# Four quarters of the array at once: a unit's second head pair beside its first

## The chip, the cores and the metric

The kernel runs on one core of a Trainium2 chip, as one program. Its time is the device time of that core in microseconds (us). TensorE has an array of 128 rows by 128 columns. A product whose operands lie on 64 partitions and whose result has 64 columns of weights uses one quarter of it: the rows are those of the operands' partitions, the columns decide on which partitions of PSUM the result lands. Which two quarters a pair of such products uses, and whether four products use all four, is what is changed here.

## The reference, cut to what matters

One layer of a decoder trunk for 256 prompt tokens and 32 sample tokens (8 sequences of 4). One input projection feeds 8 retention heads and 32 RWKV-7 heads of 64; one output projection follows. The change touches the RWKV-7 group only:

```python
def rwkv7_recurrence(r, w, k, v, kk, a, s0):
    def step(s, inp):
        r_t, w_t, k_t, v_t, kk_t, a_t = inp
        sa = jnp.einsum('bhvk,bhk->bhv', s, -kk_t)
        s = (s * w_t[:, :, None, :] + sa[..., None] * (kk_t * a_t)[:, :, None, :]
             + v_t[..., None] * k_t[:, :, None, :])
        return s, jnp.einsum('bhvk,bhk->bhv', s, r_t)
...
    o_rw, s_rwkv_new = rwkv7_recurrence(r_h, heads(decay), k_h, v_h, kk, heads(a), s_rwkv.astype(f32))
    o_rw = group_norm(o_rw, RWKV_GN_EPS) * ... + jnp.sum(r_h * k_h * r_k, axis=-1, keepdims=True) * v_h
```

Everything is float32.

## The kernel before

Three stretches follow one another: a front that computes the modulation (`ada`) and the normalised input, eight units that each hold the input projection of four RWKV heads and of one retention head, and the output projection. The projections are large products on the whole array (tile `acc`), with weights cut into a high and a low part (`whi` by ScalarE, `wlo` by VectorE or GpSimd) and three products a block.

A unit `q` of `rwkv_blocks` has two head pairs, `p` = 0 and 1. A pair's channels lie on the 128 partitions: head `h` = 0 on 0 to 63, `h` = 1 on 64 to 127 (`hs2`). The tokens are cut into nine chunks `c` of 32 (eight of the prompt, the ninth holds the sample tokens). The steps of a unit are generators that the planner interleaves with the projection's blocks:

- `main_gen`: builds `AR` and `BK` (channels on partitions), then the chunk products `scp` (line 838), whose masked result `SC` has tokens on partitions; turns `v` into token rows (`UV`, lines 849 to 854); the products `avp` (line 866) give `XR`.
- `inv_gen`: inverts the 32 by 32 triangles of the eight prompt chunks on VectorE, ended by the products `iva` and `ivb` (lines 961 to 974). `turn_gen` turns `BK` into token rows `BKt`.
- `chain_gen` (line 978): the recurrence over the eight prompt chunks, three groups of products a chunk in the tiles `ch` (`AR` by the state `S`, `WT` by `XR`, `BKt` by `UV`), for both pairs in each group.
- `sample_gen(p)` (line 1041), one for each pair: the ninth chunk with its eight states: `xps`, three times `ups`, `sps`.
- `out_gen` (line 1081): the products `ops` (line 1091), the norm of each head, and the turn back to channels, into `y`.

In all of these products head 0 reads partitions 0 to 63 (or a part of them) and writes PSUM partitions 0 to 63, and head 1 reads and writes 64 to 127, for both pairs: two quarters on a diagonal of the array. A float32 product on TensorE shows as two matmul records.

The order of the instructions is set when the program is built. `account` (line 196) keeps a simulated clock for each engine, and `c_pe` (line 212) gives each product's price; `tick` (line 287) lets a generator go on when its results are due by that clock, holds those that stopped at `PART` until two are held or one has waited 0.8 us, and lets `CHAIN` go at once. Each engine then runs its instructions strictly in that order. PSUM tiles come from three rings: `acc` (3 buffers), `tp` (3 buffers, `tps`), `ch` (2 buffers, used by the chain).

Of the kernel before, what the change touches and what calls it, by code (L numbers as in the profile page):

```python
# [10 lines left out]
F32 = mybir.dt.float32  # L11
# [6 lines left out]
P = 128  # L18
# [3 lines left out]
NB = 8  # L22
# [79 lines left out]
def tile_hybrid_step(  # L102
# [30 lines left out]

    def tt(eng, out, in0, in1, op):
        eng.tensor_tensor(out=out, in0=in0, in1=in1, op=op)
# [74 lines left out]
    small, weight = [False], [1.0]  # L210

    def c_pe(name, a, k):
        n, m, kk = free(a[0]), a[0].shape[0], a[1].shape[0]
        switch = 0.08 if small[0] and n >= 256 else 0.0
        small[0] = n < 128
        weight[0] = 0.3 if m <= 64 and kk <= 64 and n <= 64 else 1.0
        if m == 32 and n == 256 and kk == P:
            return 0.12 + switch
        passes, cyc = (1, 2) if name == "transpose" else (2, 2) if a[2].dtype == F32 else (1, 1)
        if m <= 64 and kk <= 64 and n == 512:  # L220
            return passes * 0.215
        if m <= 64 and kk <= 64 and n <= 64:
            return passes * (n * cyc / 2.4e3 + m / 2.4e3) / 2 + (0.02 if kk == 32 else 0.005 if passes == 2 else 0)
        return passes * (max(n * cyc / 2.4e3, m * 0.00084) + 0.0025) + switch
# [457 lines left out]
    def rwkv_blocks(q):  # L682
# [95 lines left out]
        def main_gen():  # L778
# [52 lines left out]
            flat = lambda t: t.rearrange("p a t -> p (a t)")  # L831
            for p in range(2):
                yield PART
                for c0, c1, m0 in ((0, 8, 0), (8, 9, 64)):
                    scp = tps("scp")
                    for c in range(c0, c1):
                        for h in hs2:
                            mm(scp[h, 64 * (c - c0):64 * (c - c0) + 64], flat(BK[h, p, c]), flat(AR[h, p, c]))
                    n = c1 - c0
                    tt(V, SC[:, p, c0:c1, :], scp[:, 0:64 * n].rearrange("p (c t) -> p c t", t=64),  # L840
                       mk[:, m0:m0 + 64].unsqueeze(1).to_broadcast([P, n, 64]), MUL)
                yield from pace(SPC)
# [6 lines left out]
            for p in range(2):  # L849
                V.transpose(UV[:, p, :, 32:64], c9(vw[:, p, :]))  # L850
                yield
                for h in range(2):
                    S.copy(UV[quad(h, 1), p, :, 0:32], UV[quad(h, 0), p, :, 32:64])
                yield
# [3 lines left out]
            B["XR"] = XR  # L858
            for p in range(2):
                yield PART  # L860
                for c0, c1 in ((0, 8), (8, 9)):
                    avp = tps("avp")
                    for c in range(c0, c1):
                        for h in hs2:
                            v = slice(h.start + 32, h.stop)
                            mm(avp[h, 64 * (c - c0):64 * (c - c0) + 64], SC[v, p, c, :], UV[v, p, c, :])
                    act(XR[:, p, c0:c1, :].rearrange("p c k -> p (c k)"), avp[:, 0:64 * (c1 - c0)], AF.Copy,
                        scale=K("amask"))
                yield from pace(SPC)
            yield from wait(("inv", q), ("bkt", q))  # L870
            B["s0"] = mx.tile([P, 2, NB, 64], F32, tag="b4", name="s0")
            B["xs"] = rwp.tile([P, 2, 64], F32, tag="MR", name="xs")
            for p in range(2):
                spawn(sample_gen(p), 2 + p)
            yield from chain_gen()
            yield from wait(("smp", q, 0), ("smp", q, 1), ("bps", q))
# [29 lines left out]
        def turn_gen(BK, BKt):  # L906
            for a in range(2):
                V.transpose(BKt[:, :, :, 32 * a:32 * a + 32], BK[:, :, :, a, :])
                yield
            for h in range(2):  # L910
                low, high = BKt[quad(h, 0), :, :, 32:64], BKt[quad(h, 1), :, :, 0:32]
                sw = B["zt"][96:128, 0:576].rearrange("t (p c k) -> t p c k", p=2, c=9)
                S.copy(sw, low)
                S.copy(low, high)
                S.copy(high, sw)
                yield
            flag(("bkt", q))
# [60 lines left out]
        def chain_gen():  # L978
# [5 lines left out]
            for c in range(NC):  # L984
                if c > 0:
                    for p in range(2):
                        for h in hs2:
                            mm(chs[p][h, 0:64], AR[h, p, c].rearrange("p a t -> p (a t)"), St[p][h, :])
                        tt(V, XR[:, p, c, :], chs[p][:, 0:64], XR[:, p, c, :], ADD)
                    yield CHAIN  # L990
                for p in range(2):
                    for a in ha2:
                        mm(chs[p][a, 64:128], WT[a, p, c, :], XR[a, p, c, :])
                    S.copy(UV[0:32, p, c, :], chs[p][0:32, 64:128])
                    V.tensor_copy(UV[64:96, p, c, :], chs[p][64:96, 64:128])
                yield CHAIN
                for p in range(2):
                    for h in hs2:
                        mm(chs[p][h, 128:192], BKt[h, p, c, :], UV[h, p, c, :])
                    sn = rwp.tile([P, 64], F32, tag=f"S{p}", name=f"S{p}", bufs=2)  # L1000
                    d = dec[p][:, c:c + 1]
                    if c == 0:
                        ts(V, sn, chs[p][:, 128:192], d, None, MUL)
                    else:
                        stt(sn, chs[p][:, 128:192], d, SP[p], MUL, ADD)
                    St[p] = sn
                    if c < NC - 1:
                        sp = rwp.tile([P, 64], F32, tag=f"SP{p}", name=f"SP{p}")
                        ts(V, sp, sn, dec[p][:, c + 1:c + 2], None, MUL)
                        SP[p] = sp  # L1010
                yield CHAIN
# [29 lines left out]
        def sample_gen(p):  # L1041
# [4 lines left out]
            s0r = B["s0r"][p]  # L1046
            s0, xs_, uvm = B["s0"][:, p], B["xs"][:, p], s0r.rearrange("p b v k -> p b (v k)")
            V.transpose(fl(s0), s0r.rearrange("p b v k -> p (b v k)"))
            yield PART
            xps = tps("xps")  # L1050
            for h in hs2:
                mm(xps[h], AR[h, p, 8].rearrange("p a t -> p (a t)"), fl(s0)[h])
            tt(V, uvm, xps.rearrange("p (b v) -> p b v", b=NB), bm, MUL)
            V.tensor_reduce(out=xs_, in_=uvm.rearrange("p b v -> p v b"), axis=AX.X, op=ADD)
            tt(V, XR[:, p, 8, :], XR[:, p, 8, :], xs_, ADD)
            tt(V, s0, s0, dec[p][:, 8:16].unsqueeze(2).to_broadcast([P, NB, 64]), MUL)
            yield PART
            for it in range(3):
                ups = tps("ups")
                src = XR if it == 0 else UV  # L1060
                for a in ha2:
                    mm(ups[a, 0:64], SC[a, p, 8, 0:CH], src[a, p, 8, :])
                for a in ha2:
                    tt(V, UV[a, p, 8, :], ups[a, 0:64], XR[a, p, 8, :], ADD)
                yield PART if it < 2 else None
            tt(G, uvm, UV[:, p, 8, :].unsqueeze(1).to_broadcast([P, NB, 64]), bm, MUL)
            yield PART
            sps = tps("sps")
            for h in hs2:
                mm(sps[h], BKt[h, p, 8, :], fl(uvm)[h])  # L1070
            tt(V, uvm, sps.rearrange("p (b v) -> p b v", b=NB),
               dec[p][:, 8:16].unsqueeze(2).to_broadcast([P, NB, 64]), MUL)
            yield
            tt(V, fl(s0), fl(s0), fl(uvm), ADD)
            yield
            V.transpose(s0r.rearrange("p b v k -> p (b v k)"), fl(s0))
            yield
            spawn(state_out(p, s0r))
            flag(("smp", q, p))

        def out_gen():
            SC, UV, XR = B["SC"], B["UV"], B["XR"]
            bst = rwp.tile([P, 18, 6], F32, tag="bst", name="bst")
            gst = rwp.tile([P, 3, 18], F32, tag="gst", name="gst")
            for p in range(2):
                yield PART
                for c0, c1 in ((0, 8), (8, 9)):
                    ops = tps("ops")
                    for c in range(c0, c1):
                        for h in hs2:  # L1090
                            mm(ops[h, 64 * (c - c0):64 * (c - c0) + 64], SC[h, p, c, :], UV[h, p, c, :])
                    xv = XR[:, p, c0:c1, :].rearrange("p c k -> p (c k)")
                    tt(V, xv, ops[:, 0:64 * (c1 - c0)], xv, ADD)
                yield from pace(SPC)
# [19 lines left out]
            for p in range(2):  # L1114
# [4 lines left out]
                for h in range(2):  # L1119
                    S.copy(o[quad(h, 0), :, 32:64], o[quad(h, 1), :, 0:32])  # L1120
                yield
                V.transpose(c9(on), o[:, :, 32:64])
# [434 lines left out]
```

## Time and profile before

| | |
|---|---|
| median of 3 runs | 1619.37 us (1618.7 to 1621.46) |
| the profiled execution's own time | 1622.13 us |
| its span, from the first to the last instruction | 1620.3 us |
| mean granted TensorE clock | 0.971 |
| TensorE, VectorE, ScalarE, GpSimd busy | 94%, 73%, 46%, 25% |

Busy time of an engine is the time in which at least one of its instructions was under way. Matmul records overlap, so the step from one start to the next says what a product costs, and its own duration does not. `x8` behind a row of the timeline is a count of records merged into it.

### The profile page before, as it was taken

The numbers are of one execution on the slowest core, as the hardware profiler recorded it, in microseconds if no ns is written. First come the engines' busy times: TensorE is split into PE (matmuls) and PEld (weight loads), VectorE is DVE, ScalarE is ACT, GpSimd is POOL, SyncE is SP. The second block draws the span as 40 slices with busy tenths as digits, with TensorE's granted clock in tenths as the row PEclk, the third lists the DMA queues.
The fourth block names the chain that finished last, engine by engine and source line by source line (L and its number), as shares of the span: only waits on it lengthen the run. The fifth ranks groups of instructions, "written<-read, shape, count | busy, mean of one in ns | idle before, by whom it ended". The sixth has DMA issues, their size and how long they took to land. (4 is left out here: it accounts for less than half of the span.)

```text
span 1620.3 us, 37403 instructions
## 1 busy us (share of the span) xinstructions
PE 1516.8 (94%) x14194; PEld 1341.9 (83%) x14194; DVE 1177.4 (73%) x2981; ACT 745.3 (46%) x1610; POOL 404.2 (25%) x425
## 2 busy tenths in 40 slices
PE   4889899999999999999999999999899999799996
PEld 2777897897889778878897898789878987699996
DVE  2434878998688869886888698878868986754544
ACT  2224453463446344534453455344543654454443
POOL 0001323422132214222412241324323422210100
PEclk8799999999999999999999999999999999999998
DMA  9995654664656456635674565365527543575553
GB/s 294 339 347 176 190 150 138 181 194 122 171 175 190 118 164 189 187 107 160 201 194 115 162 167 162 91 182 162 150 81 194 158 144 99 158 227 171 161 162 114
DMA packets 347761, 277.30 MB, mean 171 GB/s; under 512 B 90270, under 2 KB 346110, under 8 KB 346868
## 3 DMA queue, kind: packets, MB, share of 16 engines
q1 hardware_dynamic: 347580, 274.91, 58.4%
q8 instruction: 111, 1.82, 0.5%
q14 instruction: 70, 0.57, 0.1%
HBM read 248.80 MB, written 26.03 MB: 170 GB/s over the span
## 5 line engine op out<-in xcount | busy, mean ns | idle before, releaser
L249 PE MATMUL acc<-Hhi,whi 128*128 128x288 f32 (+2 forms) x2080 | 621.5, 313 | 17.2 <-DVE y L249 7.0
L249 PE MATMUL acc<-Hlo,whi 128*128 128x288 f32 (+2 forms) x2080 | 624.1, 311 | 0.0
L249 ACT CAST whi<-raw 128x512 fp32r<-128x512 f32 (+1 forms) x648 | 394.3, 617 | 404.9 <-PE acc L249 303.1
L249 PE MATMUL acc<-Hhi,wlo 128*128 128x288 f32 (+2 forms) x2080 | 458.6, 302 | 14.1 <-DVE wlo L249 13.4
L249 PEld LDWEIGHTS acc<-Hhi,whi 128*128 128x128 f32 (+1 forms) x2080 | 399.8, 192 | 52.5 <-issue 28.9
L249 POOL TENSOR_TENSOR wlo<-raw,whi 128x512 fp32r<-128x512 f32 x180 | 246.4, 1372 | 784.2 <-ACT whi L249 583.1
L249 DVE TENSOR_TENSOR wlo<-raw,whi 128x512 fp32r<-128x512 f32 (+1 forms) x468 | 337.2, 726 | 137.4 <-ACT whi L249 131.7
L249 PEld LDWEIGHTS acc<-Hlo,whi 128*128 128x128 f32 (+1 forms) x2080 | 399.5, 192 | 20.3 <-issue 8.1
L249 PEld LDWEIGHTS acc<-Hhi,wlo 128*128 128x128 f32 (+1 forms) x2080 | 341.9, 192 | 20.0 <-DVE wlo L249 18.3
L249 PE MATMUL acc<-yhi,whi 128*128 128x288 f32 x480 | 136.0, 299 | 7.4 <-ACT yhi L249 6.9
L249 PE MATMUL acc<-ylo,whi 128*128 128x288 f32 x480 | 136.0, 298 | 0.2 <-DVE ylo L249 0.2
L249 PE MATMUL acc<-yhi,wlo 128*128 128x288 f32 x480 | 101.4, 297 | 0.1
L249 PEld LDWEIGHTS acc<-yhi,whi 128*128 128x128 f32 x480 | 90.9, 189 | 8.1 <-ACT yhi L249 7.1
L249 PEld LDWEIGHTS acc<-ylo,whi 128*128 128x128 f32 x480 | 90.8, 189 | 0.7 <-DVE ylo L249 0.5
L249 PEld LDWEIGHTS acc<-yhi,wlo 128*128 128x128 f32 x480 | 76.8, 190 | 0.4 <-POOL wlo L249 0.3
L249 PE MATMUL adaps<-raw,cT 128*32 128x256 f32 x768 | 57.5, 419 | 7.2 <-DMA raw<-in_w_ada_dram 6.4
L249 DVE SCALAR_TENSOR_TENSOR s0b<-s0b,ups 128x512 f32<-128x512 f32 x64 | 40.9, 681 | 12.4 <-PE ups L249 12.4
L249 DVE SCALAR_TENSOR_TENSOR S<-ch,dec,SP 128x64 f32<-128x64 f32 x112 | 30.6, 279 | 24.7 <-PE ch L249 23.6
L249 PEld LDWEIGHTS adaps<-raw,cT 128*32 128x32 f32 x768 | 20.9, 116 | 30.4 <-DMA raw<-in_w_ada_dram 13.5
L249 ACT COPY UV<-ch 32x64 f32<-32x64 f32 x128 | 20.0, 198 | 53.6 <-PE ch L249 51.7
L249 DVE TENSOR_SCALAR SP<-S,dec 128x64 f32<-128x64 f32 x112 | 40.3, 360 | 4.0
L249 POOL TENSOR_TENSOR rot<-rot,rt 128x288 f32<-128x288 f32 x32 | 31.8, 1015 | 40.5 <-DVE rt L249 40.5
(250 smaller groups left out, 1989.4 us busy)
## 6 DMA issues: line engine op xcount, KB each, us to landing
raw<-in_w_in_dram SPq DMA_DIRECT2D x512, 256.0 KB, 2.9
raw<-in_w_ada_dram SPq DMA_DIRECT2D x64, 512.0 KB, 8.5
raw<-in_w_out_dram SPq DMA_DIRECT2D x128, 256.0 KB, 3.1
raw<-in_w_ada_dram SPq DMA_DIRECT2D x64, 256.0 KB, 3.1
s0b<-in_state_ret_dram SPq DMA_DIRECT2D x64, 256.0 KB, 4.3
out_dram<-s0b SPq DMA_DIRECT2D x64, 256.0 KB, 3.1
y<-in_x_prompt_dram SPq DMA_DIRECT2D x4, 1024.0 KB
s0r<-in_state_rwkv_dram SPq DMA_DIRECT2D x128, 32.0 KB, 2.8
```

What stands on the lines that cost most here:

```text
L249: return f(*a, **k)
```

## The change: the second pair takes the other diagonal

For `p` = 1 the token rows hold the heads in exchanged halves: head 0's tokens on partitions 64 to 127, head 1's on 0 to 63. A product from channels to tokens, or back, then has its operands on one half and its result on the other, so the second pair uses the other two quarters. `mm4` marks such products, and the planner's price of one is multiplied by 0.55. The two pairs' products of a step are issued together, in two banks. The other edits: `scp`, `avp` and `ops` take the two `ch` buffers and do both pairs in one step; the copies that put token rows in place are made anew (`turn_gen` builds the second pair's rows in `UV` as scratch, so `main_gen` waits for it before it fills `UV`); `sample_gen` does both pairs in one generator.

```diff
+    def mm4(out, lhsT, rhs):
+        four[0] = True
+        T.matmul(out, lhsT, rhs, start=True, stop=True)
+        four[0] = False
...
+        par = 0.55 if four[0] else 1.0
         if m <= 64 and kk <= 64 and n == 512:
-            return passes * 0.215
+            return par * passes * 0.215
...
-            for p in range(2):
-                yield PART
-                for c0, c1, m0 in ((0, 8, 0), (8, 9, 64)):
-                    scp = tps("scp")
-                    for c in range(c0, c1):
-                        for h in hs2:
-                            mm(scp[h, 64 * (c - c0):64 * (c - c0) + 64], flat(BK[h, p, c]), flat(AR[h, p, c]))
...
+            yield PART
+            scps, sc8 = [pch.tile([P, 512], F32, tag="ch", name="scp") for p in range(2)], [tps("scp") for p in range(2)]
+            for c in range(9):
+                for p in range(2):
+                    for h in range(2):
+                        o = hs2[h ^ p]
+                        t = scps[p][o, 64 * c:64 * c + 64] if c < 8 else sc8[p][o, 0:64]
+                        mm4(t, flat(BK[hs2[h], p, c]), flat(AR[hs2[h], p, c]))
...
-            for p in range(2):
-                V.transpose(UV[:, p, :, 32:64], c9(vw[:, p, :]))
-                yield
-                for h in range(2):
-                    S.copy(UV[quad(h, 1), p, :, 0:32], UV[quad(h, 0), p, :, 32:64])
+            yield from wait(("turn", q))
+            V.transpose(UV[:, 0, :, 32:64], c9(vw[:, 0, :]))
+            yield
+            for h in range(2):
+                S.copy(UV[quad(h, 1), 0, :, 0:32], UV[quad(h, 0), 0, :, 32:64])
+            yield
+            tq = rwp.tile([P, NR], F32, tag="tq", name="tq")
+            V.transpose(tq, vw[:, 1])
+            yield
+            for h in range(2):
+                for i in range(2):
+                    S.copy(UV[quad(1 - h, 1), 1, :, 32 * i:32 * i + 32], c9(tq)[quad(h, i)])
                 yield
...
+            avps, av8 = [pch.tile([P, 512], F32, tag="ch", name="avp") for p in range(2)], tps("avp")
...
         def turn_gen(BK, BKt):
+            T2 = B["UV"][:, 1]
             for a in range(2):
-                V.transpose(BKt[:, :, :, 32 * a:32 * a + 32], BK[:, :, :, a, :])
+                s = slice(32 * a, 32 * a + 32)
+                V.transpose(T2[:, :, s], BK[:, 1, :, a, :])
+                V.transpose(BKt[:, 0, :, s], BK[:, 0, :, a, :])
                 yield
             for h in range(2):
-                low, high = BKt[quad(h, 0), :, :, 32:64], BKt[quad(h, 1), :, :, 0:32]
-                sw = B["zt"][96:128, 0:576].rearrange("t (p c k) -> t p c k", p=2, c=9)
+                for i in range(2):
+                    for a in range(2):
+                        S.copy(BKt[quad(1 - h, a), 1, :, 32 * i:32 * i + 32], T2[quad(h, i), :, 32 * a:32 * a + 32])
+                    yield
+            flag(("turn", q))
+            for h in range(2):
+                low, high = BKt[quad(h, 0), 0, :, 32:64], BKt[quad(h, 1), 0, :, 0:32]
+                sw = c9(B["zt"][96:128, 0:288])
                 S.copy(sw, low)
                 S.copy(low, high)
                 S.copy(high, sw)
...
-                        for h in hs2:
-                            mm(chs[p][h, 0:64], AR[h, p, c].rearrange("p a t -> p (a t)"), St[p][h, :])
+                        for h in range(2):
+                            mm4(chs[p][hs2[h ^ p], 0:64], AR[hs2[h], p, c].rearrange("p a t -> p (a t)"), St[p][hs2[h], :])
+                    for p in range(2):
                         tt(V, XR[:, p, c, :], chs[p][:, 0:64], XR[:, p, c, :], ADD)
...
-                        mm(chs[p][a, 64:128], WT[a, p, c, :], XR[a, p, c, :])
+                        mm4(chs[p][a.start + 32 * p:a.stop + 32 * p, 64:128], WT[a, p, c, :], XR[a, p, c, :])
...
-                        mm(chs[p][h, 128:192], BKt[h, p, c, :], UV[h, p, c, :])
+                        mm4(chs[p][hs2[h ^ p], 128:192], BKt[hs2[h], p, c, :], UV[hs2[h], p, c, :])
...
-        def sample_gen(p):
+        def sample_gen():
...
+            xps = [tps("xps") for p in range(2)]
+            for p in range(2):
+                for h in range(2):
+                    mm4(xps[p][hs2[h ^ p]], AR[hs2[h], p, 8].rearrange("p a t -> p (a t)"), fl(s0s[:, p])[hs2[h]])
...
-                    mm(ups[a, 0:64], SC[a, p, 8, 0:CH], src[a, p, 8, :])
-                for a in ha2:
-                    tt(V, UV[a, p, 8, :], ups[a, 0:64], XR[a, p, 8, :], ADD)
+                    tt(V, UV[a, :, 8, :], ups[a, 0:128].rearrange("p (c v) -> p c v", c=2), XR[a, :, 8, :], ADD)
...
+            sps = [tps("sps") for p in range(2)]
...
+            ops, op8 = [pch.tile([P, 512], F32, tag="ch", name="ops") for p in range(2)], tps("ops")
...
                 for h in range(2):
-                    S.copy(o[quad(h, 0), :, 32:64], o[quad(h, 1), :, 0:32])
-                yield
-                V.transpose(c9(on), o[:, :, 32:64])
+                    S.copy(o[quad(h, 0), :, 32 - 32 * p:64 - 32 * p], o[quad(h ^ p, 1), :, 0:32])
+                yield
+                if p == 1:
+                    for h in range(2):
+                        S.copy(o[quad(h, 1), :, 0:32], o[quad(1 - h, 1), :, 32:64])
+                    yield
+                V.transpose(c9(on), o[:, :, 32 - 32 * p:64 - 32 * p])
```

The rows and counts of `avp`, `ups` and `ops` products stay as they were (`mm`, two quarters); only their grouping changes.

## Rows read from the trace of the kernel before

**Rows 1.** The page: busy us, share of the span and instructions of each engine.

```profile
PE 1516.8 (94%) x14194; PEld 1341.9 (83%) x14194; DVE 1177.4 (73%) x2981; ACT 745.3 (46%) x1610; POOL 404.2 (25%) x425
```

**Rows 2.** Busy time by stretch: the sixth unit, its chain, the stretch before a scp.

```profile
927.00:1082.00 155.00, 149.60 (x1469) 133.30 (x1464) 128.85 (x332) 76.87 (x163) 45.13 (x46) 1.00 0.55 153
...
1022.00:1074.00 52.00, 51.48 (x477) 40.09 (x474) 39.19 (x112) 20.98 (x58) 13.37 (x20) 1.00 0.45 119
...
1082.00:1124.00 42.00, 39.68 (x294) 38.46 (x291) 40.20 (x105) 18.74 (x34) 23.66 (x16) 0.96 0.60 165
```

**Rows 3.** Waits of TensorE, the longest kind: us in total, times, longest.

```profile
PE acc L249 <- DVE wlo L249: 13.4, 12, 3.0
```

**Rows 4.** Groups of TensorE's instructions by shape: count, busy, mean ns of one.

```profile
L249 PE MATMUL scp<-AR,BK 64*64 64x64 f32 x576 | 20.2, 221 | 0.0
...
L249 PE MATMUL xps<-s,AR 64*64 64x512 f32 x64 | 16.1, 592 | 0.0
```

**Rows 5.** Timeline of TensorE around one pair's scp: start, us.

```profile
1274.55 0.43 PE L249 MATMUL acc<-Hhi,wlo 128*128 128x288 f32 x2
1274.91 1.26 PE L249 MATMUL scp<-AR,BK 64*64 64x64 f32 x36
1276.10 0.40 PE L249 MATMUL acc<-Hhi,whi 128*128 128x288 f32 x1
1276.34 0.30 PE L249 MATMUL acc<-Hlo,whi 128*128 128x288 f32 x1
1276.47 0.30 PE L249 MATMUL acc<-Hhi,whi 128*128 128x288 f32 x1
```

**Rows 6.** Timeline of TensorE: a chain group, then an ups group.

```profile
1203.21 0.45 PE L249 MATMUL ch<-S,AR 64*64 64x64 f32 x8
1203.59 0.30 PE L249 MATMUL ups<-UV,SC 32*32 32x64 f32 x4
1203.82 0.40 PE L249 MATMUL acc<-Hlo,whi 128*128 128x296 f32 x1
```

**Rows 7.** Timeline of TensorE: both pairs' xps in one piece.

```profile
243.32 1.93 PE L249 MATMUL xps<-s,AR 64*64 64x512 f32 x8
245.19 0.40 PE L249 MATMUL acc<-Hlo,whi 128*128 128x288 f32 x1
```

**Rows 8.** Timeline of TensorE: retention products on column quarters, then row quarters.

```profile
272.31 1.07 PE L249 MATMUL rcr<-s0b,qp 128*32 128x256 f32 x16
273.19 0.61 PE L249 MATMUL rcr<-vf,scq 128*32 128x256 f32 x8
273.74 0.50 PE L249 MATMUL ups<-kv 32*128 32x256 f32 x4
274.17 0.40 PE L249 MATMUL acc<-Hhi,whi 128*128 128x296 f32 x1
```

**Rows 9.** The chain that ended last: start, us, what.

```profile
1151.61 1.19 PE avp L249 x36
...
1180.29 0.90 PE ivb L249 x64
...
1359.16 0.86 PE rop L249 x4
```

**Rows 10.** Groups of ScalarE and VectorE that the token rows take: busy us, mean ns.

```profile
L249 ACT COPY UV<-UV 32x288 f32<-32x288 f32 x32 | 13.8, 430 | 11.9 <-DVE UV L249 11.3
...
L249 ACT COPY BKt<-BKt 32x576 f32<-32x576 f32 x16 | 10.7, 671 | 0.5
...
L249 DVE TENSOR_TENSOR UV<-ups,XR 32x64 f32<-32x64 f32 x96 | 20.6, 215 | 1.7
...
L249 DVE STREAM_TRANSPOSE BKt<-BK 128x576 f32<-128x576 f32 x16 | 11.9, 746 | 0.0
...
L249 DVE STREAM_TRANSPOSE UV<-vw 128x288 f32<-128x288 f32 x16 | 7.5, 469 | 0.0
```

**Rows 11.** Timeline of VectorE behind the scp of rows 5.

```profile
1277.39 0.81 DVE L249 TENSOR_TENSOR SC<-scp,cst 128x512 f32<-128x512 f32 x2
```

More of the change, by code (lines that the diff above doesn't have):

```diff
@@ L208, in free @@
         return n
-    small, weight = [False], [1.0]
+    small, weight, four = [False], [1.0], [False]
     def c_pe(name, a, k):
@@ L219, in c_pe @@
         passes, cyc = (1, 2) if name == "transpose" else (2, 2) if a[2].dtype == F32 else (1, 1)
+        par = 0.55 if four[0] else 1.0
         if m <= 64 and kk <= 64 and n == 512:
-            return passes * 0.215
+            return par * passes * 0.215
         if m <= 64 and kk <= 64 and n <= 64:
-            return passes * (n * cyc / 2.4e3 + m / 2.4e3) / 2 + (0.02 if kk == 32 else 0.005 if passes == 2 else 0)
+            return par * passes * (n * cyc / 2.4e3 + m / 2.4e3) / 2 + (0.02 if kk == 32 else 0.005 if passes == 2 else 0)
         return passes * (max(n * cyc / 2.4e3, m * 0.00084) + 0.0025) + switch
@@ L831, in main_gen @@
             flat = lambda t: t.rearrange("p a t -> p (a t)")
-            for p in range(2):
-                yield PART
-                for c0, c1, m0 in ((0, 8, 0), (8, 9, 64)):
-                    scp = tps("scp")
-                    for c in range(c0, c1):
-                        for h in hs2:
-                            mm(scp[h, 64 * (c - c0):64 * (c - c0) + 64], flat(BK[h, p, c]), flat(AR[h, p, c]))
[L839 to L842, printed above, removed]
+            yield PART
[6 more added lines that the diff above has]
+                        mm4(t, flat(BK[hs2[h], p, c]), flat(AR[hs2[h], p, c]))
+            for p in range(2):
+                tt(V, SC[:, p, 0:8, :], scps[p].rearrange("p (c t) -> p c t", t=64),
+                   mk[:, 0:64].unsqueeze(1).to_broadcast([P, 8, 64]), MUL)
+                tt(V, SC[:, p, 8, :], sc8[p][:, 0:64], mk[:, 64:128], MUL)
+            yield from pace(SPC)
             B["zt"] = mx.tile([P, 1056], F32, tag="b4", name="zt")
@@ L858, in main_gen @@
             B["XR"] = XR
+            yield PART
+            avps, av8 = [pch.tile([P, 512], F32, tag="ch", name="avp") for p in range(2)], tps("avp")
             for p in range(2):
[L860 to L863, printed above, removed]
-                        for h in hs2:
[L865 to L869, printed above, removed]
+                for c in range(9):
+                    for h in hs2:
+                        v = slice(h.start + 32, h.stop)
+                        t = avps[p][h, 64 * c:64 * c + 64] if c < 8 else av8[h, 64 * p:64 * p + 64]
+                        mm(t, SC[v, p, c, :], UV[v, p, c, :])
+            for p in range(2):
+                act(XR[:, p, 0:8, :].rearrange("p c k -> p (c k)"), avps[p], AF.Copy, scale=K("amask"))
+            act(XR[:, :, 8, :], av8[:, 0:128].rearrange("p (a k) -> p a k", a=2), AF.Copy, scale=K("amask"))
+            yield from pace(SPC)
             yield from wait(("inv", q), ("bkt", q))
-            B["s0"] = mx.tile([P, 2, NB, 64], F32, tag="b4", name="s0")
-            B["xs"] = rwp.tile([P, 2, 64], F32, tag="MR", name="xs")
-            for p in range(2):
-                spawn(sample_gen(p), 2 + p)
+            spawn(sample_gen(), 2)
             yield from chain_gen()
-            yield from wait(("smp", q, 0), ("smp", q, 1), ("bps", q))
+            yield from wait(("smp", q), ("bps", q))
             yield from out_gen()
@@ L986, in chain_gen @@
                     for p in range(2):
-                        for h in hs2:
-                            mm(chs[p][h, 0:64], AR[h, p, c].rearrange("p a t -> p (a t)"), St[p][h, :])
+                        for h in range(2):
+                            mm4(chs[p][hs2[h ^ p], 0:64], AR[hs2[h], p, c].rearrange("p a t -> p (a t)"), St[p][hs2[h], :])
+                    for p in range(2):
                         tt(V, XR[:, p, c, :], chs[p][:, 0:64], XR[:, p, c, :], ADD)
@@ L992, in chain_gen @@
                     for a in ha2:
-                        mm(chs[p][a, 64:128], WT[a, p, c, :], XR[a, p, c, :])
-                    S.copy(UV[0:32, p, c, :], chs[p][0:32, 64:128])
-                    V.tensor_copy(UV[64:96, p, c, :], chs[p][64:96, 64:128])
+                        mm4(chs[p][a.start + 32 * p:a.stop + 32 * p, 64:128], WT[a, p, c, :], XR[a, p, c, :])
+                for p in range(2):
+                    S.copy(UV[0:32, p, c, :], chs[p][32 * p:32 * p + 32, 64:128])
+                    V.tensor_copy(UV[64:96, p, c, :], chs[p][64 + 32 * p:96 + 32 * p, 64:128])
                 yield CHAIN
                 for p in range(2):
-                    for h in hs2:
-                        mm(chs[p][h, 128:192], BKt[h, p, c, :], UV[h, p, c, :])
+                    for h in range(2):
+                        mm4(chs[p][hs2[h ^ p], 128:192], BKt[hs2[h], p, c, :], UV[hs2[h], p, c, :])
+                for p in range(2):
                     sn = rwp.tile([P, 64], F32, tag=f"S{p}", name=f"S{p}", bufs=2)
@@ L1045, in sample_gen @@
             fl = lambda t: t.rearrange("p b v -> p (b v)")
-            s0r = B["s0r"][p]
-            s0, xs_, uvm = B["s0"][:, p], B["xs"][:, p], s0r.rearrange("p b v k -> p b (v k)")
-            V.transpose(fl(s0), s0r.rearrange("p b v k -> p (b v k)"))
-            yield PART
[L1050 to L1056, printed above, removed]
+            ob = lambda t: t.rearrange("p (b v) -> p b v", b=NB)
+            s0s = mx.tile([P, 2, NB, 64], F32, tag="b4", name="s0")
+            xs_ = rwp.tile([P, 2, 64], F32, tag="MR", name="xs")
+            uvm = [t.rearrange("p b v k -> p b (v k)") for t in B["s0r"]]
+            dcs = [dec[p][:, 8:16].unsqueeze(2).to_broadcast([P, NB, 64]) for p in range(2)]
+            for p in range(2):
+                V.transpose(fl(s0s[:, p]), fl(uvm[p]))
+                yield
+            yield PART
+            xps = [tps("xps") for p in range(2)]
+            for p in range(2):
+                for h in range(2):
+                    mm4(xps[p][hs2[h ^ p]], AR[hs2[h], p, 8].rearrange("p a t -> p (a t)"), fl(s0s[:, p])[hs2[h]])
+            for p in range(2):
+                tt(V, uvm[p], ob(xps[p]), bm, MUL)
+            yield
+            for p in range(2):
+                V.tensor_reduce(out=xs_[:, p], in_=uvm[p].rearrange("p b v -> p v b"), axis=AX.X, op=ADD)
+                yield
+            tt(V, XR[:, :, 8, :], XR[:, :, 8, :], xs_, ADD)
             yield PART
@@ L1060, in sample_gen @@
                 src = XR if it == 0 else UV
+                for p in range(2):
+                    for a in ha2:
+                        mm(ups[a, 64 * p:64 * p + 64], SC[a, p, 8, 0:CH], src[a, p, 8, :])
                 for a in ha2:
-                    mm(ups[a, 0:64], SC[a, p, 8, 0:CH], src[a, p, 8, :])
-                for a in ha2:
-                    tt(V, UV[a, p, 8, :], ups[a, 0:64], XR[a, p, 8, :], ADD)
+                    tt(V, UV[a, :, 8, :], ups[a, 0:128].rearrange("p (c v) -> p c v", c=2), XR[a, :, 8, :], ADD)
                 yield PART if it < 2 else None
-            tt(G, uvm, UV[:, p, 8, :].unsqueeze(1).to_broadcast([P, NB, 64]), bm, MUL)
+            for p in range(2):
+                tt(G, uvm[p], UV[:, p, 8, :].unsqueeze(1).to_broadcast([P, NB, 64]), bm, MUL)
+                tt(V, s0s[:, p], s0s[:, p], dcs[p], MUL)
+                yield
             yield PART
[L1068 to L1072, printed above, removed]
-            yield
-            tt(V, fl(s0), fl(s0), fl(uvm), ADD)
-            yield
[L1076 to L1079, printed above, removed]
+            sps = [tps("sps") for p in range(2)]
+            for p in range(2):
+                for h in range(2):
+                    mm4(sps[p][hs2[h ^ p]], BKt[hs2[h], p, 8, :], fl(uvm[p])[hs2[h]])
+            for p in range(2):
+                tt(V, uvm[p], ob(sps[p]), dcs[p], MUL)
+            yield
+            for p in range(2):
+                tt(V, s0s[:, p], s0s[:, p], uvm[p], ADD)
+                yield
+                V.transpose(fl(uvm[p]), fl(s0s[:, p]))
+                yield
+                spawn(state_out(p, B["s0r"][p]))
+            flag(("smp", q))
         def out_gen():
@@ L1084, in out_gen @@
             gst = rwp.tile([P, 3, 18], F32, tag="gst", name="gst")
+            yield PART
+            ops, op8 = [pch.tile([P, 512], F32, tag="ch", name="ops") for p in range(2)], tps("ops")
             for p in range(2):
[L1086 to L1094, printed above, removed]
+                for c in range(9):
+                    for h in hs2:
+                        t = ops[p][h, 64 * c:64 * c + 64] if c < 8 else op8[h, 64 * p:64 * p + 64]
+                        mm(t, SC[h, p, c, :], UV[h, p, c, :])
+            for p in range(2):
+                xv = XR[:, p, 0:8, :].rearrange("p c k -> p (c k)")
+                tt(V, xv, ops[p], xv, ADD)
+            tt(V, XR[:, :, 8, :], op8[:, 0:128].rearrange("p (a k) -> p a k", a=2), XR[:, :, 8, :], ADD)
+            yield from pace(SPC)
             flag(("ops", q))
@@ L1119, in out_gen @@
                 for h in range(2):
-                    S.copy(o[quad(h, 0), :, 32:64], o[quad(h, 1), :, 0:32])
+                    S.copy(o[quad(h, 0), :, 32 - 32 * p:64 - 32 * p], o[quad(h ^ p, 1), :, 0:32])
                 yield
-                V.transpose(c9(on), o[:, :, 32:64])
+                if p == 1:
+                    for h in range(2):
+                        S.copy(o[quad(h, 1), :, 0:32], o[quad(1 - h, 1), :, 32:64])
+                    yield
+                V.transpose(c9(on), o[:, :, 32 - 32 * p:64 - 32 * p])
                 yield
```

## Prediction

> **What bounds the kernel now.** I read the page first: TensorE is busy 94% of the span, VectorE 73%, ScalarE 46% [rows 1]. Then the busy time by stretch: in a unit of 155 us TensorE has work under way for 149.6 us and VectorE for 128.9; in that unit's chain, where the touched products are, it is 51.5 and 39.2 of 52 us [rows 2]. The waits of TensorE agree: the longest kind, for the low part of the weights, is 13.4 us in all [rows 3]. So TensorE, which runs its queue in order, sets the time, and a step that it no longer spends is gained as long as VectorE keeps up. It nearly doesn't ahead of a `scp` (40.2 of 42 us, [rows 2]), but no product of the change lies there.
>
> **What a round costs.** The shapes show that the touched products use a quarter each and come as records of 64 columns (`scp`, 576 of them) or of 512 (`xps`, 64 of them) [rows 4]. From one group's start to the next group's: 36 records of `scp` take 1.19 us (1274.91 to 1276.10) [rows 5], 8 records of a chain group 0.38 (1203.21 to 1203.59) [rows 6]. Both have the same entry and exit, so the 14 rounds of two records between them cost 0.81 us: a round of two is 0.058 us, and 0.148 us a group is fixed. For `xps`, 8 records take 1.87 us [rows 7]; less 0.148, a round of two is 0.43 us. Do two records really share a round? A float32 record of 256 columns on the whole array takes 0.86 / 4 = 0.215 us (`rop`, [rows 9]), so 512 columns take 0.43: yes, the round of two costs what one record does.
>
> **Would four share it?** No row has four quarters of 64 by 64. The two things that are new have a row each. Two products on the same rows: `rcr` has four records at a time on all 128 rows in four column strips, 16 of them in 0.88 us, 0.22 for four of 256 columns [rows 8], the price of one. Two products that write the same PSUM partitions, in two banks: the retention's `ups`, 32 rows by all 128 columns, take 0.43 us for four records up to the next start [rows 8]. An `acc` record takes 0.13 for 288 columns (1276.34 to 1276.47, [rows 5]), so four of 256 columns in turn would need 0.46 without entry and exit; two at a time need 0.23, and leave 0.20 for these. So both kinds overlap, and I take full overlap: a round of four costs 0.058, or 0.43 for the long ones. The other end is no overlap, nothing gained a round.
>
> Nor does issue forbid it: `ivb` has 64 records, each with a weight load, in 0.90 us, 14 ns a record [rows 9], so four need 56 ns, just under the round of 58. The Trainium skill speaks against this point: in "TensorE: Matmul & The Clock Gate", Back-to-back issue gap, a matmul of up to 64 columns has a floor of about 25 ns, by which a round of four would take 0.100 us and save 0.016 of the two rounds' 0.116, not 0.058; the short rounds below would then save 8 us in all in place of 30, and the sum would end at 1598 us. The 14 ns of the row contradict that floor.
>
> **The sum, a unit.** Rounds saved: `scp` has 9 chunks for two pairs, 36 rounds of two, then 18 of four: 18. The chain groups go from 4 rounds to 2: 7 chunks with `AR`, 8 with `WT`, 8 with `BKt`: 14 + 16 + 16. That is 64 rounds by 0.058 = 3.71 us. `xps` and `sps` go from 4 long rounds to 2 each: 4 by 0.43 = 1.72. `scp`, `avp` and `ops` each go into the projection's stream once in place of twice. Such an insertion costs, beside its rounds, 0.10 on the way in (two `acc` records from 1274.55 would end their steps at 1274.81; `scp` starts at 1274.91), the fixed 0.148 and 0.11 on the way out (the first `acc` step is 0.24, later ones 0.13) [rows 5]: 0.36, three times 1.08. The sample's `ups` go from six groups to three; a group of 4 records takes 0.23, of which two rounds are 0.116 [rows 6], so 0.114 falls away three times: 0.34. Together 6.85 us a unit, 54.8 us for eight.
>
> **What it adds.** ScalarE, a unit: before, 8 copies of 288 columns at 0.43 and 6 of 576 at 0.67, 7.5 us; after, 6 for `UV`, 14 in `turn_gen`, 6 in the output at 0.43, 11.2 us [rows 10]; 3.7 more, 30 us in all, on an engine with 875 us free [rows 1]. What is late is `avp`: it now stands behind 8 of the copies, four turns of 0.47 and two more copies in `UV`, 6.2 us. It is covered by the inversion, which the chain needs too: an `avp` that starts at 1151.6 has 27.5 us from its end to the `ivb` at 1180.3 [rows 9]. I take 0; uncovered it would be 6.2 by 8 = 50 us. VectorE, a unit: four turns at 0.47 for two at 0.75 add 0.39; six fewer `ups` sums at 0.215, with the rest twice as wide, give back between 0 and 1.29 [rows 10]. Nothing either way.
>
> Two costs are waits of which the trace before has no row. First, the same work of VectorE falls into less time: 128.9 of 155 us become 128.9 of 148, 83% to 87% [rows 2]. Below, this costs nothing, since the chain's stretch has 13 us of VectorE free and loses 5 or less; above, I allow 2 us a unit; I take 1, 8 us in all. Second, the last chunk of `scp`, the `xps` and the `sps` now hold two of the three `tp` buffers at once. The products behind them in TensorE's queue, the retention's and the projection's alike, wait if they need a third. A buffer is held from the end of `scp` (1276.10, [rows 5]) to the end of its masking (1277.39 + 0.81, [rows 11]), 2.1 us; three such places in eight units are 50 us if each wait is whole, 0 if the third buffer does. Because other steps take one buffer at a time, I take 0.5 us a unit, 4 us.
>
> 54.8 - 8 - 4 = 42.8. The profiled execution took 1622.1 us (1620.3 of span and 1.8 around it), so 1579.3; it stands 2.8 above the median of the runs shown, so **1577 us** at their level. Its own range is 1562 (no added wait, and a few us for an order that the planner, with other prices, makes anew) to 1594 (30 us of added waits).
>
> **The rivals.**
>
> *The quarters take turns.* If two products on one half of the rows or of the PSUM partitions can't run together once all four quarters are in use, the 64 short and 4 long rounds save nothing. There remain 1.08 + 0.34 a unit, 11 us, less some 6 of added waits: 1614. Against it are rows 8, each for one half of the condition; no row has both. The Trainium skill would have it so: "TensorEngine Tiling (Array Packing)", Restrictions and Gotchas, says that different row tiles can't access the same PSUM bank simultaneously, and here both row halves write each bank. The trace disagrees already before the change: the two heads of a `scp` are two row halves that write one bank, and share a round of 0.058.
>
> *Issue binds.* If a record needs not 14 but 28 ns, four take what two rounds took, and only the long rounds and the insertions are left: 1.72 + 1.42 a unit, 25 us, less 12: 1606. Rows 9 speak against it, though 56 against 58 ns leaves little.
>
> *The waits eat half.* Full overlap, but `tp` buffers and VectorE cost 35 us in place of 12: 1600. For it: VectorE's 87%, and a planner that knows of no buffers. Against it: 13.4 us for the largest wait now [rows 3].
>
> *Slower: a change of diagonal drains the array.* A change of shape costs some 0.10 us [rows 5]. If going from one diagonal to the other counts as one, then each of a unit's 34 groups of eight records (9 + 7 + 8 + 8 + 1 + 1) pays at least twice: 68 by 0.10 is 6.8 us, less 1.42, plus 1.5 of waits, 55 us in eight units: 1674. The 1.42 and the waits cancel, so it decides from 0.006 us a change on (3 us in eight units). Against it: in rows 8 neither four column strips nor two row strips pay anything between them.
>
> **How the numbers follow.** Forecast 0.68 (1577), waits eat half 0.14 (1600), turns 0.09 (1614), issue 0.05 (1606), slower 0.04 (1674). The range 1560 to 1606 leaves out the turns, the slower case and the tails, under 0.2. A measurement of this kernel tells 0.2%, some 3 us, from no change. Faster: the first, second and fourth whole, and half of the third, 0.92; same 0.04, the rest of the third; slower 0.04.
>
> **What would show it.** One `scp` group of 72 records a unit from start to next start in about 1.2 us (2.2 if they take turns), with four records starting within some 25 ns and the next four 58 ns later; chain groups of 8 records at 0.26 us in place of 0.38; `xps` of 8 records at 1.0 in place of 1.87; `acc` records as many and as long as before. Wrong would be: TensorE waiting at `adat`, `rtp` or `rop` for a `tp` buffer behind `xps`; `avp` ending later than `ivb`; a granted clock under 1.0 in more stretches than before [rows 2], since the pauses between shorter groups stay.

## The result and the profile after

The changed kernel took 1579.2 us in the median (1576.7 to 1585.1) against 1620.4 before, a ratio of 0.975 with a 95% interval of 0.972 to 0.978: faster by 2.5%. The forecast was 1577.

The new rounds first. TensorE's timeline around the `scp` of the sixth unit, around a chain group and around `xps`, to be read beside [rows 5 to 7]:

```profile
952.00 0.29 PE L255 MATMUL acc<-Hhi,whi 128*128 128x288 f32 x1
952.23 1.28 PE L255 MATMUL scp<-AR,BK 64*64 64x64 f32 x72
953.43 0.40 PE L255 MATMUL acc<-Hlo,whi 128*128 128x288 f32 x1
...
241.98 0.34 PE L255 MATMUL ch<-S,AR 64*64 64x64 f32 x8
242.25 0.40 PE L255 MATMUL acc<-Hhi,whi 128*128 128x288 f32 x1
...
391.18 0.34 PE L255 MATMUL ch<-S,AR 64*64 64x64 f32 x8
391.34 1.04 PE L255 MATMUL xps<-s,AR 64*64 64x512 f32 x8
392.31 0.40 PE L255 MATMUL acc<-Hhi,whi 128*128 128x288 f32 x1
```

72 records of `scp` take 1.20 us from start to next start (36 took 1.19), 8 chain records 0.27 (0.38), 8 `xps` records 0.97 (1.87). Inside the first group four records start within 20 ns; the second four start 106 ns after the first, and from there on a round follows every 58 ns. So a round of four costs what a round of two did.

Now the balance. The page's first row and the cores' row of the kernel after:

```profile
PE 1473.6 (93%) x14194; PEld 1311.4 (83%) x14194; DVE 1170.0 (74%) x2899; ACT 777.7 (49%) x1698; POOL 442.8 (28%) x459
```
```profile
core 0: 1583.3 us, clock 0.967
```

Idle time of TensorE is span less busy time. What the granted clock withheld is the span by 1 less the mean clock. Busy time less that is called step time here: what the products would keep TensorE busy at full clock (pauses shorter than a record, some 0.2 us, hide in it).

| profiled execution | span | idle | withheld | step time |
|---|---|---|---|---|
| before | 1620.3 | 103.5 | 47.0 | 1469.8 |
| after | 1583.3 | 109.7 | 52.2 | 1421.4 |

So in this pair 48.4 us of step time went, and 11.4 came back: 6.2 as waits, 5.2 as clock. Two things limit this reading.

- It charges the clock also with time at 1.2 GHz in which TensorE had nothing to do (9 to 10 us of it behind the last product). TensorE was busy in 76.3 us of the time at 1.2 GHz before and in 79.9 after; its products lost half of that, 38.1 and 40.0. By this strict count 44.9 us of step time went, 6.2 came back as waits and 1.8 as clock. Kernels with the same products on the same quarters lie up to 8 us apart in step time by the first count and up to 3 by the strict one, so the strict figure is added below where it matters.
- The profiled execution after was the slowest of its four. The withheld time by the first count is 50.1 us in the mean of these four, and 50.4 in the mean of 33 executions of the kernel before that were timed beside the experiments. So over all executions the clock took nothing back that can be told.

TensorE's longest waits, where [rows 3] had 13.4 us for the low parts of the weights, and one that became shorter (here us in total, times, longest):

```profile
PE acc L255 <- DVE wlo L255: 22.5, 24, 2.6
PE acc L255 <- ACT yhi L255: 10.4, 1, 10.4
PE ch L255 <- DVE XR L255: 1.3, 3, 0.7
```

The same two waits in the kernel before:

```profile
PE ch L249 <- DVE XR L249: 8.9, 12, 1.8
PE acc L249 <- ACT yhi L249: 6.9, 1, 6.9
```

The wait for `yhi` stands where the output projection needs the result `y` of the last unit.

How the clock stood behind a wait is seen in the busy time by stretch of the kernel after. The last columns are the granted clock, the share of the DMA engines and GB/s:

```profile
660.00:670.00 10.00, 6.78 (x46) 4.99 (x44) 8.63 (x19) 5.88 (x13) 3.27 (x3) 0.99 0.62 190
670.00:682.00 12.00, 12.00 (x112) 11.86 (x113) 7.16 (x17) 3.55 (x7) 0.00 (x0) 0.58 0.32 89
```

TensorE had work for 6.8 of 10 us (one wait of 2.4 us, at an `adat`), and then ran most of the next 12 us at 1.2 GHz of 2.4.

### The profile page after: what moved, and what is told of

Read it like the earlier page. It is cut to its first block, busy times and chain, and to the rows that moved or that the text cites. A ratio compares the mean times of both kernels' runs of the same rounds, so it can differ in the third digit from the quotient of the medians.

```text
span 1583.3 us, 37468 instructions
## 1 busy us (share of the span) xinstructions
PE 1473.6 (93%) x14194; PEld 1311.4 (83%) x14194; DVE 1170.0 (74%) x2899; ACT 777.7 (49%) x1698; POOL 442.8 (28%) x459
## 5 line engine op out<-in xcount | busy, mean ns | idle before, releaser
L255 PE MATMUL acc<-Hlo,whi 128*128 128x288 f32 (+2 forms) x2080 | 617.7, 309 | 0.0
L255 POOL TENSOR_TENSOR wlo<-raw,whi 128x512 fp32r<-128x512 f32 x214 | 290.6, 1361 | 753.2 <-ACT whi L255 524.7
L255 PEld LDWEIGHTS acc<-Hlo,whi 128*128 128x128 f32 (+1 forms) x2080 | 399.4, 192 | 14.6 <-issue 5.7
L255 DVE TENSOR_TENSOR wlo<-raw,whi 128x512 fp32r<-128x512 f32 (+1 forms) x434 | 315.1, 731 | 126.9 <-ACT whi L255 122.3
L255 DVE COPY UV<-ch 32x64 f32<-32x64 f32 x128 | 28.9, 226 | 31.9 <-ACT UV L255 28.7
L255 ACT COPY UV<-ch 32x64 f32<-32x64 f32 x128 | 25.5, 199 | 41.4 <-PE ch L255 39.7
L255 DVE TENSOR_SCALAR SP<-S,dec 128x64 f32<-128x64 f32 x112 | 38.1, 340 | 4.0
```

What stands on the lines that cost most here:

```text
L255: return f(*a, **k)
```

## The experiments

Each was timed several times over, in turn with the kernel before (medians 1622.6 to 1623.0 there). Ratios are to it, with their 95% intervals. "Strictly" marks step time by the strict count.

**one_diagonal: the same order, without the quarters.**

```diff
-                        o = hs2[h ^ p]
+                        o = hs2[h]
...
-                            mm4(chs[p][hs2[h ^ p], 0:64], AR[hs2[h], p, c]...
+                            mm4(chs[p][hs2[h], 0:64], AR[hs2[h], p, c]...
```
and alike for `WT`, `BKt`, `xps` and `sps`.

> The changed kernel with its grouping, copies and order of instructions kept to the letter, but every mm4 product of the second pair put in the first pair's quarters (the planner's prices kept too). The second pair's results are then not those of the reference. Overlap theory (four quarters at once make the gain): 64 short rounds by 0.058 us and 4 long ones by 0.43 come back in each of eight units, 43 us; 1579 + 43 = 1622 us, with chain groups of 8 records at 0.38 us again and xps of 8 records at 1.85. Rival (the grouping, fewer insertions and fewer changes of shape, makes the gain and the quarters take turns): within 5 us of the changed kernel, 1574 to 1584.

1605.4 us, 0.989 (0.987 to 0.991). Neither number: 26 us above the changed kernel, where the theory had 43 and the rival under 5. The order is the same: in the two traces the same instructions follow one another on every engine (all but 4 of TensorE's 14194 records). The rounds themselves did come back, as its timeline shows (72 records of `scp` in 2.24 us):

```profile
965.33 2.31 PE L255 MATMUL scp<-AR,BK 64*64 64x64 f32 x72
967.57 0.40 PE L255 MATMUL acc<-Hlo,whi 128*128 128x288 f32 x1
```

Its page and cores' row, and its first wait:

```profile
PE 1501.8 (94%) x14194; PEld 1337.0 (83%) x14194; DVE 1167.1 (73%) x2899; ACT 771.8 (48%) x1698; POOL 444.0 (28%) x459
```
```profile
core 0: 1602.6 us, clock 0.969
```
```profile
PE acc L255 <- DVE wlo L255: 17.7, 21, 2.6
```

Step time 1452.1, so the quarters take away 30.7 us (strictly 32.1); idle 100.8 against 109.7, so 8.9 of that came back as waits.

**grouping_alone: the other half of the change, as a kernel.** `o = hs2[h]` and alike, the copies and turns of the kernel before, price 1.0; the grouping kept.

> The grouping without the quarters, as a kernel of its own that computes the reference: both pairs in one step of scp, avp, ops and of the sample, but the second pair's token rows, copies and quarters as before, and the planner's prices as before. Overlap theory: 1.42 us a unit for insertions and ups groups, 11 us, less some waits for tp buffers; 1609 to 1617 us. Rival (grouping makes the gain): 1575 to 1590.

1608.7 us, 0.991 (0.989 to 0.993): at the lower end of the theory's range, 14.0 us below the kernel before. Its page and cores' row:

```profile
PE 1506.8 (94%) x14194; PEld 1340.9 (84%) x14194; DVE 1176.7 (73%) x2901; ACT 744.9 (46%) x1602; POOL 432.7 (27%) x441
```
```profile
core 0: 1605.4 us, clock 0.966
```

Step time 1506.8 busy less 54.6 withheld = 1452.2, the same as one_diagonal's; the grouping takes away 17.6 us (strictly 15.1), more than the 11.4 of the sum.

**long_rounds_back: only xps and sps return.**

```diff
-                    mm4(xps[p][hs2[h ^ p]], ...
+                    mm4(xps[p][hs2[h]], ...
```
and `sps` alike.

> The changed kernel with only xps and sps of the second pair put back in the first pair's quarters, which gives that pair's sample results wrong values. Overlap theory: 4 long rounds of 0.43 us a unit come back, 13.8 us; 1593 us. Rival (the sample's products are covered by the waits of the chain that runs beside them, so a long round is worth less than its length): under 7 us, 1579 to 1586.

1589.8 us, 0.980 (0.978 to 0.982), some 10 us above the changed kernel: between the theory's 14 and the rival's 7, so the time alone does not decide. The records do: the steps that follow `xps` records add up to 14.6 us here and 7.9 in the changed kernel, 0.84 a unit where the sum had 0.86; those of `sps` to 15.2 and 9.7, only 0.69 a unit. That is 12.3 us, close to the theory.

**inverse_quarters: two more kinds of products on four quarters.**

```diff
+            for c in range(NC):
+                for p in range(2):
+                    for a in ha2:
+                        i = NC * p + c
+                        mm4(ps[a.start + 32 * p:a.stop + 32 * p, HB * c:HB * c + HB], SC[a, p, c, 0:CH], MR[a, i, :])
```
and `ivb` alike, each with its copies out by pair.

> The changed kernel, and iva and ivb too put the second pair on column quarters beside the first (output 32 partitions further), each evacuated by one copy a pair. Overlap theory: 16 rounds of 0.031 us and 16 of 0.028 fall away a unit, 0.95 us, 7.6 us in all, less two more copies on ScalarE and three on VectorE a unit; 1571 to 1576 us. Rival (the issue of 14 ns a record binds these short records, so four in a round cost two rounds): 1579 to 1583, with ivb records still 14 ns apart.

1579.3 us, 0.973 (0.971 to 0.975): no gain that can be told, as the rival had it. Yet the records share rounds, as the theory said (timeline of TensorE):

```profile
229.67 0.73 PE L255 MATMUL iva<-MR,SC 32*32 32x16 f32 x64
230.33 0.40 PE L255 MATMUL acc<-Hlo,whi 128*128 128x288 f32 x1
...
232.29 0.68 PE L255 MATMUL ivb<-WT,itmp 32*16 32x16 f32 x64
232.90 0.40 PE L255 MATMUL acc<-Hhi,whi 128*128 128x288 f32 x1
```

64 `ivb` records in 0.61 us, 9.5 ns each with entry and exit; inside, a round of four starts every 25 to 34 ns, 6 to 8 ns a record. So issue doesn't bind at 14 ns, and the rival falls by its own condition. The steps of `iva` and `ivb` add up to 11.0 us here and to 15.7 in the changed kernel: 4.7 of the 7.6 that the theory had. Step time as a whole fell by 9.9 us (1458.8 busy less 47.3; strictly 7.4), idle time rose by 7.6 to 117.3.

**quarters_no_copies: is ScalarE's new work covered?** grouping_alone with the `mm4` outputs and the price of the change.

> grouping_alone with only the quarters added: the second pair's mm4 products go to the other diagonal, at the planner's lower price, but the copies that exchange its halves, the wait for them and the scratch turns are left out, so its values are wrong. It is the changed kernel without what the change adds to ScalarE. If the copies are covered, as the prediction's sum has it: 1575 to 1581 us, as the changed kernel. Rival (the copies and the longer end of the last unit cost part of the gain): 1565 to 1573.

1587.5 us, 0.978 (0.976 to 0.980): not faster than the changed kernel but 8 us slower, outside both ranges. No cost of the copies shows. But the order of its instructions is another one too, and orders of the same work lie 7 to 8 us apart (old_price below), so a cost of that size can't be ruled out. Its idle time is 111.4, as in the changed kernel; the clock is 0.963, 58.7 us withheld against 52.2.

**light_inverse and light_inverse_diagonal: VectorE relieved.**

```diff
-            for j in range(1, HB - 1):
+            for j in (1, 2):
```

> The changed kernel with 2 of the 14 steps of the inversion's loop (so the inverse is not one): 24 of 28 VectorE instructions a unit left out, some 6 us a unit. Made to be compared with light_inverse_diagonal. Theory (VectorE, which falls behind where the loop runs, gives back 9 us or more of what the quarters save): light_inverse lies 32 us or more below light_inverse_diagonal, against 26 between the changed kernel and one_diagonal. Rival (the loss lies elsewhere): 22 to 29 us below.

> one_diagonal with the same 2 of 14 steps: same order as light_inverse, the second pair's products in the first pair's quarters. Theory: 32 us or more above light_inverse. Rival: 22 to 29 us above.

1565.0 us (0.965, 0.963 to 0.967) and 1596.3 (0.984, 0.982 to 0.986): 31.4 apart, just under the theory's bound and above the rival's range. The traces are clearer; page and cores' row of light_inverse, then of light_inverse_diagonal:

```profile
PE 1466.9 (94%) x14194; PEld 1306.9 (84%) x14194; DVE 1113.2 (71%) x2726; ACT 783.4 (50%) x1698; POOL 424.7 (27%) x440
PE 1498.5 (94%) x14194; PEld 1333.5 (84%) x14194; DVE 1111.9 (70%) x2726; ACT 778.4 (49%) x1698; POOL 423.9 (27%) x440
```
```profile
core 0: 1559.8 us, clock 0.973
core 0: 1594.2 us, clock 0.975
```

Idle is 92.9 with the quarters and 95.7 without (it was 109.7 and 100.8 with the whole loop), and the step times are 1424.8 and 1458.6, 33.8 apart (strictly 36.1). With VectorE relieved nothing of the quarters' saving returns as waits.

**old_price: what the planner believes.**

```diff
-        par = 0.55 if four[0] else 1.0
+        par = 1.0
```

> The changed kernel with the planner's old price for mm4 products (1.0 for 0.55); it computes the reference. The planner then leaves up to 5 us a unit more of simulated TensorE time, so steps that wait for a due time come a little later in the queue. If the order matters little: 1575 to 1584 us. Rival (the planner's price makes part of the gain, or its lower price makes the waits): more than 5 us above, or below, the changed kernel.

1572.5 us, 0.969 (0.967 to 0.971): the rival, by a little, and the faster kernel, though a price of 0.55 is nearer to what the rounds cost. Page, cores and the stretches beside those shown of the changed kernel:

```profile
PE 1459.1 (93%) x14194; PEld 1299.0 (83%) x14194; DVE 1176.3 (75%) x2913; ACT 780.3 (50%) x1698; POOL 438.9 (28%) x445
```
```profile
core 0: 1570.0 us, clock 0.977
```
```profile
660.00:670.00 10.00, 8.36 (x66) 7.71 (x66) 8.86 (x24) 7.98 (x17) 2.01 (x2) 1.00 0.85 258
670.00:682.00 12.00, 12.00 (x146) 11.77 (x145) 10.09 (x24) 7.59 (x15) 1.44 (x2) 1.00 0.44 128
```

Step time 1423.0 and idle 110.9 are those of the changed kernel to 2 us; only the clock differs: 36.1 us withheld against 52.2 (39.6 against 50.1 in the mean of each kernel's four executions). In these 22 us it ran 212 records of products where the changed kernel ran 158.

**changed_again and old_price_diagonal: is that real?**

> The changed kernel once more, on the chip of old_price's kin, to see whether old_price (0.9687 of the time before) is truly below it (0.975): 1576 to 1584 us, half clock for over 40 us after 150 us again. If the half clock varies from execution to execution and not with the order: under 1575.

1580.4 us, 0.973 (0.971 to 0.976), clock 0.966, as expected. The longer stretches at 1.2 GHz returned in the same places (from 526, 670 and 1366 us on, where the changed kernel had 527, 670 and 1370), and the withheld time is 49.9 in the mean of five executions. So they belong to the order and not to one execution:

```profile
670.00:682.00 12.00, 12.00 (x114) 11.86 (x115) 6.79 (x15) 3.99 (x8) 0.00 (x0) 0.60 0.30 88
```

> one_diagonal with the planner's old price: the order of old_price, the second pair's products in the first pair's quarters, its values wrong. The step time that the quarters take away is the same at either price, 34 us between one_diagonal and the changed kernel without waits and half clock; waits give back some 10: 1594 to 1602 us, 22 to 30 above old_price. Rival (old_price gains because its order suits the quarters better): over 32 us above old_price, 1605 or more.

1596.2 us, 0.983 (0.981 to 0.986), 23.7 above old_price, as the theory had it. Step time 1492.9 busy less 38.3 (clock 0.976) = 1454.6, 31.6 above old_price (strictly 32.0); 9.4 us of it returned as waits (idle 101.5 against 110.9). So the quarters are worth the same at either price.

**old_price_pool and old_price_inverse: going on from there.** `VC = 0.5` for 1.0; and inverse_quarters at price 1.0.

> old_price with the planner's bound VC at 0.5 in place of 1.0 us: more of the low parts of the weights go to GpSimd, and VectorE's queue is shorter; it computes the reference. If the waits for the low parts (16.9 us in old_price) come from VectorE's queue: 1563 to 1569 us, with under 13 us of them. Rival (GpSimd takes 1.36 us for what VectorE does in 0.73, so a part that goes there comes later): 1571 to 1580.

1604.9 us, 0.989 (0.986 to 0.992): far above both ranges. GpSimd took 255 low parts at 1.38 us in place of 200, and the waits for low parts fell to 12.5 us, as expected; but idle time rose to 126.0 (12.2 us at `adat` for VectorE, where old_price has 3.8), and 57.7 us were withheld. A wait that was shortened in one place came out in others; what moved them was not traced further.

> old_price and inverse_quarters in one kernel that computes the reference: planner's price 1.0 for mm4, iva and ivb on four quarters. If old_price's gain is the granted clock (23.9 us at half clock after 150 us, 54.6 in the changed kernel, with equal waits) and inverse_quarters' saving of steps was eaten by waits, the two add up only where the new order keeps the clock: 1562 to 1570 us. Rival (each new order draws its waits and its clock anew, with some 8 us to either side): 1570 to 1582.

1566.9 us, 0.966 (0.963 to 0.969), within the theory's range: the fastest of the kernels that leave nothing out, though its interval overlaps that of old_price. It is 12.3 us below the changed kernel (1579.2).

## Why the prediction was right, step by step

- **Four share a round.** Right, to the 58 ns. The bank rule of "TensorEngine Tiling (Array Packing)" in the Trainium skill (Restrictions and Gotchas) does not hold here: both row halves write each bank, and four records still share a round. Turns, drains between the diagonals and an issue limit all fall by the `scp` row. The 25 ns floor of "TensorE: Matmul & The Clock Gate" in the Trainium skill (Back-to-back issue gap) fell in inverse_quarters, where four records start in 25 to 34 ns.
- **The quarters' term, 43.4 us.** The mechanism is right, the size too large; of the sum this is the step that missed by most. Three pairs of kernels with one order each give 30.7, 33.8 and 31.6 us of step time (strictly 32.1, 36.1 and 32.0). An undisturbed group saves 1.04 us at `scp`, 0.10 in the chain and 0.845 each at `xps` and `sps`: with 23 chain groups a unit, 40.4 us in eight units. A chain group saves 0.10 and not 0.116, since in its last round two more records start, 6 to 7 ns each. Added up over the whole traces, the steps of these six kinds of groups fell by 36.9, 36.7 and 34.2 us (strictly, same order of pairs): the other 4 to 6 us are in groups that took longer than an undisturbed one. The last 1 to 5 us lie in products that the change doesn't touch, and stay open.
- **The grouping's term, 11.4 us.** Too small: 17.6 of step time (strictly 15.1), 14.0 of time. The sum of the two terms, 54.8, stands against 48.4 (strictly 44.9).
- **ScalarE's copies at nothing.** No cost shows in quarters_no_copies, which can't tell one below some 8 us. The cover shrank far more than the 6.2 us of the sum: in the seventh unit `avp` ends 12 us ahead of `ivb`, where 27.5 stood before [rows 9] and 31 in quarters_no_copies. It was still enough.
- **Waits of 12 us.** Too large: idle time rose by 6.2, and the clock, which the prediction named only among the things that could make it wrong, took 1.8 strictly in the profiled pair and nothing in the mean of all executions. The waits for the low parts from VectorE rose by 9.1 and the one for `yhi` by 3.5, while the chain's for `XR` fell by 7.6. That the part which the quarters brought, 8.9, is VectorE's is shown by the light_inverse pair. Of the 4 us for `tp` buffers one wait shows: in the seventh unit TensorE stands idle ahead of the second pair's `sps` for 1.6 us (timeline below). Behind `scp` and `xps`, where the prediction feared such waits too, none appears.
- **The order that the planner makes anew**, "a few us" in the range, is worth 7 to 8 us: old_price, with the same work and the same idle time.

The wait at that `sps` (timeline of TensorE and VectorE):

```profile
1187.99 1.08 PE L255 MATMUL sps<-s0r,BKt 64*64 64x512 f32 x4
1189.90 1.28 DVE L255 SCALAR_TENSOR_TENSOR s0b<-s0b,ups 128x512 f32<-128x512 f32 x2
1190.69 1.08 PE L255 MATMUL sps<-s0r,BKt 64*64 64x512 f32 x4 [1.62 <-issue]
```

It ends some 0.1 us after VectorE has read the first of the retention's two `ups` tiles. The profile names no releaser; by the program's order that tile holds the one of the three buffers that this `sps` needs.

So the total came out in part by luck: the quarters' term was 7 to 13 us too large, the grouping's 4 to 6 too small, and the waits some 6 too large.

## What to carry to other kernels

Where small products fill two quarters of the array, put two more on the other diagonal. Here the round was free, with each product in a quarter of its own and the two that write the same output partitions in two banks; what has to be paid for is the layout. On an engine that runs an order made ahead of time, split a change's worth into step time, waits and withheld clock before judging it, and take the clock from more executions than the profiled one: here almost a third of what the quarters saved came back as waits in two of three pairs. A new price in such a planner is a change of its own; time it by itself. Here the price nearer to the measured rounds gave the order that is 7 to 8 us slower; whether that is more than the chance of one order was not tested.

## What the runs showed of the hardware

- Four float32 products of 64 by 64 by 64 on the four quarters, two of them on the same rows and two on the same PSUM partitions, cost 58 ns a round together, what two cost.
- TensorE starts a record, with its weight load, every 6 to 8 ns where four products go to four 32 by 32 tiles of the array (16 columns, inverse_quarters).
- In the changed kernel the granted clock stood at 1.2 GHz for 3.4 to 10.2 us after waits of 1.9, 2.4 and 3.3 us (from 475, 670 and 793 us on): 0.58 in the mean over 12 us after that of 2.4. Other such stretches have no single wait of that length before them. The same program shows the longer ones in the same places again (withheld 50.1 and 49.9 us in the means), and another order of the same work withholds 39.6.
